# One encoder step on one core: the values of 32 sample tokens for three mLSTM heads, computed as an fp32 product on four column parts of TensorE

## The chip, the cores and the metric

The kernel runs on one NeuronCore of one Trainium2 chip. The metric is the time on the device of one execution, in microseconds; smaller is better. It is given as the median of several runs. Beside the runs, one execution was recorded by the hardware profiler, and all rows of a trace below are from such an execution.

## The reference

The reference is one inference step of a two-layer streaming encoder. Two groups of tokens go through the same weights: a prompt of 1024 tokens and a sample of 32 tokens, 1056 together, with 1024 features each. Layer 0 is an mLSTM mixer with four heads and an MLP, layer 1 is chunk-band attention and an MLP. The change lies in the mixer's values `v`:

```
def mlstm_mixer(u, conv_prev, C0, n0, m0, w_in, b_if, conv_w, conv_b, mhn_g, w_out, chunk_len):
    proj = u @ w_in
    qk_pre = proj[..., :2 * QK_A]
    v = proj[..., 2 * QK_A:2 * QK_A + V_A]
    o_pre = proj[..., 2 * QK_A + V_A:2 * QK_A + 2 * V_A]
...
    vh = v.astype(jnp.float32).reshape(Bsz, S, NH_A, DV_A)
...
    h, C, n, m = mlstm_scan(q, k, vh, ig, lf, C0, n0, m0, chunk_len)
```

`u` is the modulated input (1056 tokens by 1024), `w_in` the input weight (1024 by 3080), and each head's values are 256 columns of it. All of it is float32.

## The kernel before

All large products are made from split operands. A float32 array is split into a high part and a rest, both in the type fp32r (`split`, L85 to L90: the high part is a cast on ScalarE, the rest a subtraction on VectorE), and a product is the sum of three matmuls: high by high, high by rest, rest by high. The tile `U` holds both parts of `u` with the features on the partitions: 8 chunks of 128 features, 1056 tokens each, and 96 zero columns behind them.

A weight is fetched by `wtile` (L92 to L104): a DMA on SyncE's queue brings 512 rows into a tile of the ring `raw` (three buffers), and the split writes both parts into a tile of the ring `wc` (six buffers). While the mixer runs, one of the three raw buffers is held by the accumulator of a modulation vector (`ada_acc`), so two are left for weights; the tile `cl`, through which a head's old state comes in, is taken from the same ring.

The mixer runs head by head. For heads 2 to 4 (the loop's h = 1 to 3; a head's number here is h + 1) three things are in flight at once. `qk_proj(h)` makes the head's queries and keys. `v_proj(h)` (L498 to L506) then makes its values: nine blocks of tokens, eight of 128 and a last one that holds the 32 sample tokens, and for each block 24 matmuls by `v_chunk` (L483 to L489), 8 feature chunks by 3 split terms, with 128 tokens of `U` as the stationary operand and 256 weight columns as the moving one. The last block also loads 128 columns of `U`: the 32 sample tokens and 96 columns behind them, whose rows of the result nobody reads. `v_out` (L491) copies a finished block on ScalarE from PSUM to a tile `vt`. Meanwhile the generator `mlstm(h-1)` (L639 on) does the scan of the head before, one chunk of 128 tokens at a time: scores `S` (L668, L669), numerator `num` (L686, L688), state update `cu` (L690), the normalisation on VectorE and ScalarE (`sm`, `hn`, L715 to L731), and the transposes `hT` on TensorE (L738). A `Flow` object gives the generators a tick after each block; `v_proj` calls `after(t)` behind each of its nine blocks.

The values of head 1 are made earlier by `v_first`, interleaved with the input's transposes, with the same `v_chunk`. After head 4's values comes `o_proj`, the output gate.

The order in which the program is written is not the order in which it runs. A scheduler in the build orders each engine's instructions by its own cost model, within the dependencies, so an instruction that depends on nothing late can move far. On each engine, instructions then run strictly in that order: an instruction that waits for a semaphore holds up everything behind it, on TensorE, VectorE, ScalarE, GpSimd and on SyncE's queue of DMAs alike. PSUM tiles come from small rings too: three buffers `mm` for projection blocks, two `nm` for `num` and `cu`, two `tp` for scores and transposes.

At the kernel's start `ada_mm` (L432 to L436) forms a modulation vector as fp32 products with a stationary of 32 columns, `cs`, placed on four column parts of the array by the partitions they write (0, 32, 64 and 96).

Of the kernel before, what the change touches and what calls it, by code (L numbers as in the profile page):

```python
# [8 lines left out]
F32 = mybir.dt.float32  # L9
F32R = mybir.dt.float32r  # L10
# [5 lines left out]
P = 128  # L16
D = 1024
KC = D // P
TP = 1024
TS = 32  # L20
T = TP + TS
NT = T // P + 1
# [53 lines left out]
def trunk_kernel(ctx: ExitStack, tc: tile.TileContext, a, o):  # L76
    nc = tc.nc
    flow = Flow()
    cp = ctx.enter_context(tc.tile_pool(name="const", bufs=1, reuse_waits="tile"))
# [12 lines left out]
    def wtile(name, srcs, ncols=256, pool=None, eng=None, between=None):  # L92

        raw = raw_tile([P, 4, ncols], f"raw_{name}")
        for dst, src in srcs(raw):
            nc.sync.dma_start(dst, src)
        if pool is None:
            w = ring.tile([P, 2, 4, ncols], F32R, tag="wc", name=f"w_{name}", bufs=6)
        else:
            w = pool.tile([P, 2, 4, ncols], F32R, tag="h", name=f"w_{name}", bufs=5)  # L100
        if between:
            between()
        split(w[:, 0], w[:, 1], raw, eng)
        return w  # L104

# [23 lines left out]
    nc.vector.tensor_add(sel, ident[:, 0:32], ident[:, 32:64])  # L129
    for i in (64, 96):  # L130
        nc.vector.tensor_add(sel, sel, ident[:, i:i + 32])
    ones_d = cp.tile([P, P], F32R, name="ones_d")
    nc.vector.memset(ones_d.bitcast(F32), 1.0 / D)
    eps_ln = cp.tile([P, 1], F32, name="eps_ln")
    nc.vector.memset(eps_ln, LN_EPS)
    eps_hn = cp.tile([P, 1], F32, name="eps_hn")
# [10 lines left out]
    NPT1, NPT2 = 112, 112  # L147
    pt1 = cp.tile([P, NPT1], F32, name="pt1")
    pt2 = cp.tile([P, NPT2], F32, name="pt2")
    cs = cp.tile([P, KC, 32], F32, name="cs")  # L150
    ada = cp.tile([P, NPT2, 2], F32, name="ada")
    bif = cp.tile([36, 1], F32, name="bif")
    nc.vector.memset(bif, 0.0)
# [19 lines left out]
    def mmt(name):  # L173
        return pa.tile([P, 512], F32, tag="mm", name=name, bufs=3)
# [32 lines left out]
    adaw = [ada_load(k) for k in range(4)]  # L207
# [158 lines left out]
    up_cm = tc.tile_pool(name="upool", bufs=1, side="right", reuse_waits="tile")  # L366
    upool = up_cm.__enter__()
    UF = KC * T
    U = upool.tile([P, 2 * UF + 96], F32R, name="U")
    nc.vector.memset(U[:, 2 * UF:].bitcast(F32), 0.0)  # L370

    def uap(hl, k, t0, n):
        off = hl * UF + k * T + t0
        return U[:, off:off + n]

# [56 lines left out]
    def ada_mm(k):  # L432

        for q in range(4):
            nc.tensor.matmul(ada_ps[32 * q:32 * q + 32, :512], cs[:, k, :], adaw[k][:, q * 512:(q + 1) * 512],
                             start=(k == 0), stop=(k == KC - 1))  # L436

    def ada_first():
# [31 lines left out]
    G = None  # L470
    cst = {}

    def v_weight(h, half):
# [7 lines left out]
        return wtile(f"v{h}_{half}", srcs, 264 if h == 0 else 256)  # L481

    def v_chunk(ps, ws, t, k):  # L483
        w = ws[k // 4]
        n = w.shape[-1]
        uh, ul = uap(0, k, t * P, P), uap(1, k, t * P, P)
        nc.tensor.matmul(ps[:, :n], uh, w[:, 0, k % 4, :], start=(k == 0), stop=False)
        nc.tensor.matmul(ps[:, :n], uh, w[:, 1, k % 4, :], start=False, stop=False)
        nc.tensor.matmul(ps[:, :n], ul, w[:, 0, k % 4, :], start=False, stop=(k == KC - 1))  # L489

    def v_out(ps, h, t):  # L491
        m = P if t < NT - 1 else TS
        vt = A.tile([P, 258], F32, tag="vt", name=f"vt_{h}_{t}", bufs=9)
        nc.scalar.copy(vt[:m, :256], ps[:m, :256])
        nc.gpsimd.memset(vt[:m, 256:258], 1.0)
        if h == 0:
            nc.vector.tensor_copy(bass.AP(g64.tensor, g64[:m, t, 0:4].offset, [g64[:m].ap[0], [32, 2], [1, 4]]),
                                  ps[:m, 256:264].rearrange("p (a b) -> p a b", a=2))  # L498
        return vt

    def v_proj(h, after):
        ws = [v_weight(h, half) for half in range(2)]
        vts = []
        for t in range(NT):
            ps = mmt(f"v_{h}_{t}")
            for k in range(KC):  # L506
                v_chunk(ps, ws, t, k)
            vts.append(v_out(ps, h, t))
            after(t)
        return vts  # L510

    def v_first(ws, nxt):

# [278 lines left out]
    def next_u(bi, k):  # L792
# [7 lines left out]
                        pass  # L800
        flow.tick()
    vts = [v_first(vw, next_u)]
    for t0, n in TBS:
        nc.sync.dma_start(xsp[0][:, :, t0:t0 + n], xt[:, :, t0:t0 + n])
    flow.finish()
# [68 lines left out]

    T_cm = tc.tile_pool(name="temps", bufs=1, reuse_waits="tile")
    T_ = T_cm.__enter__()

    def tmp_t(shape, name, dt=F32):
        return T_.tile(shape, dt, tag="t", name=name, bufs=5)
# [1287 lines left out]
```

## Time and profile before

| quantity | value |
|---|---|
| median of three runs | 2407.8 us (2407.55, 2407.8, 2413.93) |
| the profiled execution's own time | 2412.41 us |
| its span | 2410.6 us |
| mean granted TensorE clock | 0.995 |
| PE busy | 2342.7 us, 97% of the span |
| DVE busy | 1939.0 us, 80% |
| ACT busy | 1206.0 us, 50% |

PE is TensorE's matmul side and PEld its weight loads, DVE is VectorE, ACT is ScalarE, POOL is GpSimd and SP is SyncE with its DMA queue. The span is the time from the first to the last recorded instruction; the 1.8 us by which the profiled execution's own time is longer lies around it. In a row of the timeline the first number is the start in us from the span's start, the second the duration in us, then engine, line, operation, output and inputs, shape and count (x2 where two equal ones in a row are put together), and in brackets how long the engine sat idle before it and what ended that.

### The profile page before, as it was taken

The numbers are of one execution on the slowest core, as the hardware profiler recorded it, in microseconds if no ns is written. First come the engines' busy times: TensorE is split into PE (matmuls) and PEld (weight loads), VectorE is DVE, ScalarE is ACT, GpSimd is POOL, SyncE is SP. The second block draws the span as 40 slices with busy tenths as digits, with TensorE's granted clock in tenths as the row PEclk, the third lists the DMA queues.
The fourth block names the chain that finished last, engine by engine and source line by source line (L and its number), as shares of the span: only waits on it lengthen the run. The fifth ranks groups of instructions, "written<-read, shape, count | busy, mean of one in ns | idle before, by whom it ended". The sixth has DMA issues, their size and how long they took to land. (4 is left out here: it accounts for less than half of the span.)

```text
span 2410.6 us, 44188 instructions
## 1 busy us (share of the span) xinstructions
PE 2342.7 (97%) x17180; PEld 2250.4 (93%) x17180; DVE 1939.0 (80%) x3903; ACT 1206.0 (50%) x2454; POOL 168.1 (7%) x320
## 2 busy tenths in 40 slices
PE   7999999999999999999999999999999999899997
PEld 4999999999999999999999987789999999899997
DVE  4888766778788789989888777756998889888778
ACT  4565557278666630101147467773776777222212
POOL 0111100000000000000000224420000000000003
PEclk9999999999999999999999999999999999999999
DMA  8343222526566896675512330051486779976642
GB/s 302 120 131 103 78 89 66 177 91 206 184 198 200 279 336 230 252 261 215 183 56 89 82 93 1 10 140 59 165 278 211 259 278 335 355 256 236 224 146 73
DMA packets 284277, 424.64 MB, mean 176 GB/s; under 512 B 15384, under 2 KB 205228, under 8 KB 278948
## 3 DMA queue, kind: packets, MB, share of 16 engines
q1 hardware_dynamic: 279860, 391.48, 48.3%
q10 hardware_dynamic: 4208, 30.35, 3.1%
q8 instruction: 135, 2.21, 0.4%
q14 instruction: 74, 0.61, 0.1%
HBM read 305.96 MB, written 118.17 MB: 176 GB/s over the span
## 5 line engine op out<-in xcount | busy, mean ns | idle before, releaser
L1082 DVE SCALAR_TENSOR_TENSOR ACX<-dn,ada,ACX 128x264 f32<-128x264 f32 (+6 forms) x664 | 281.8, 447 | 83.2 <-PE dn L1452 41.1
L1452 PE MATMUL dn<-fx,wf_d 128*128 128x264 f32 x2016 | 254.1, 285 | 6.8 <-DVE ACX L1082 3.5
L1452 PEld LDWEIGHTS dn<-fx,wf_d 128*128 128x128 f32 x2016 | 248.8, 188 | 9.0 <-DVE ACX L1082 3.0
L89 ACT CAST w_dn<-raw_dn 128x1024 fp32r<-128x1024 f32 x36 | 37.7, 1050 | 282.1 <-DVE aw L279 136.9
L118 PE MATMUL dn<-hs,w_dn 128*128 128x384 f32 (+2 forms) x512 | 161.2, 315 | 0.0
L119 PE MATMUL dn<-hs,w_dn 128*128 128x384 f32 (+2 forms) x512 | 161.0, 315 | 0.0
L120 PE MATMUL dn<-hs,w_dn 128*128 128x384 f32 (+2 forms) x512 | 156.4, 314 | 1.3 <-DVE w_dn L90 1.3
L1317 PE MATMUL up<-TF,wf_u 128*128 128x264 f32 x1056 | 143.2, 285 | 3.8 <-ACT H L1320 3.8
L1317 PE MATMUL up<-U,wf_u 128*128 128x264 f32 x1056 | 140.3, 285 | 1.7 <-ACT H L1320 1.2
L1317 PE MATMUL up<-u,wf_u 128*128 128x264 f32 x1056 | 139.7, 285 | 1.3 <-ACT wf_u L89 0.7
L279 DVE SCALAR_TENSOR_TENSOR aw<-radw,cs,aw 128x512 f32<-128x512 f32 x196 | 139.5, 743 | 1.1 <-DMA radw<-in_w_ada_dram 1.1
L1317 PEld LDWEIGHTS up<-TF,wf_u 128*128 128x128 f32 x1056 | 134.4, 189 | 4.8 <-ACT H L1320 4.6
L1317 PEld LDWEIGHTS up<-U,wf_u 128*128 128x128 f32 x1056 | 133.0, 188 | 3.0 <-ACT H L1320 1.6
L1317 PEld LDWEIGHTS up<-u,wf_u 128*128 128x128 f32 x1056 | 132.9, 188 | 1.9 <-ACT wf_u L89 0.9
L118 PE MATMUL dn<-U,w_dn 128*128 128x384 f32 (+2 forms) x416 | 129.4, 312 | 0.6 <-DVE ada L304 0.6
L119 PE MATMUL dn<-U,w_dn 128*128 128x384 f32 (+2 forms) x416 | 129.4, 312 | 0.0
L120 PE MATMUL dn<-U,w_dn 128*128 128x384 f32 (+2 forms) x416 | 125.9, 313 | 0.6 <-DVE w_dn L90 0.5
L1817 ACT ACTIVATE p<-p,mx 128x576 f32<-128x576 f32 (+9 forms) x132 | 86.6, 657 | 27.5 <-DVE mx L1814 25.2
L120 PEld LDWEIGHTS dn<-hs,w_dn 128*128 128x128 f32 x512 | 96.0, 188 | 2.0 <-DVE w_dn L90 1.8
L118 PEld LDWEIGHTS dn<-hs,w_dn 128*128 128x128 f32 x512 | 96.5, 189 | 0.1
L119 PEld LDWEIGHTS dn<-hs,w_dn 128*128 128x128 f32 x512 | 96.6, 189 | 0.0
L90 DVE TENSOR_TENSOR HL<-H,HL 128x1056 fp32r<-128x1056 f32 x64 | 80.3, 1254 | 20.0 <-ACT HL L89 19.9
(403 smaller groups left out, 7111.0 us busy)
## 6 DMA issues: line engine op xcount, KB each, us to landing
hpl<-HL SPq DMA_DIRECT2D x144, 264.0 KB
rdn_u<-in_w_up_dram SPq DMA_DIRECT2D x64, 512.0 KB
hd<-HL SPq DMA_DIRECT2D x28, 1056.0 KB
fx<-hd SPq DMA_DIRECT2D x50, 528.0 KB
radw<-in_w_ada_dram SPq DMA_DIRECT2D x24, 1024.0 KB
hd<-HM SPq DMA_DIRECT2D x28, 792.0 KB
raw_up<-in_w_up_dram SPq DMA_DIRECT2D x40, 512.0 KB
raw_dn<-in_w_down_dram SPq DMA_DIRECT2D x36, 512.0 KB
```

Of the source, the lines that this page charges most:

```text
L89: nc.scalar.copy(dst_h, src)
L90: (eng or nc.vector).tensor_sub(dst_l, src, dst_h.bitcast(F32))
L118: nc.tensor.matmul(ps, wh, mov(0, k), start=(k == 0), stop=False)
L119: nc.tensor.matmul(ps, wh, mov(1, k), start=False, stop=False)
L120: nc.tensor.matmul(ps, wl, mov(0, k), start=False, stop=(k == nk - 1))
L279: nc.vector.scalar_tensor_tensor(acc[cnd], raw[:, k], sc, acc[cnd], op0=ALU.mult, op1=ALU.add)
L1082: nc.vector.scalar_tensor_tensor(xs, ps[:, off + o:off + o + mm_], gate[:, fc, cnd:cnd + 1], xs, op0=ALU.mult, op1=ALU.add)
L1317: nc.tensor.matmul(p, self.ws[w][:, wl, k], moving(f, tp, xl, k), start=first and k + n_ == 0, stop=k == 3 and n_ == 2, skip_group_check=n ...
L1452: nc.tensor.matmul(p, ws[w][:, wl, k], t[:, s0, xl], start=first and k + n_ == 0, stop=k == kg - 1 and n_ == 2, skip_group_check=not first)
L1817: nc.scalar.activation(z, z, AF.Exp, bias=mx[:, 0:1], scale=-1.0, accum_out=mx[:, 1:2])
```

## The change

The sample's block of values for heads 2 to 4 is no longer the ninth block of split matmuls. It is the first thing that `v_proj` does. `v_sample` runs, for each half of the weight, four fp32 products with the raw, unsplit weight as the moving operand (256 columns) and 32 columns `us` as the stationary one, one product for each of four feature chunks, each on a column part of its own, so that two halves are eight products and the four parts of one PSUM tile hold partial sums over two chunks each. `wtile` now passes the raw tile to `between`, and so these products are issued behind the weight's DMA and ahead of its split. `v_out` adds the parts up: the copy on ScalarE takes part 0, and three additions on VectorE of 32 by 256 from PSUM take the others. `us`, the sum of both parts of `u` for the sample tokens, is made once by one VectorE addition into the wider constant tile `cs`.

With it come smaller edits. The blocks of values live in a ring of eight `vt` and a ring of two `vs`, where there was one of nine. `v_first` still makes the sample's block with 24 split matmuls, but its stationary has 32 columns, not 128; so the 96 zero columns of `U` and their memset go. `ones_d`, a constant that the layer norms use later, is made in a later pool, by a memset after the mixer. `v_proj` gives the same nine ticks; the ninth now comes right behind the eighth.

```
-            between()
+            between(raw)
...
-    cs = cp.tile([P, KC, 32], F32, name="cs")
+    cs = cp.tile([P, KC, 2 + TS], F32, name="cs")
+    us = cs[:, :, 2:]
...
-    U = upool.tile([P, 2 * UF + 96], F32R, name="U")
-    nc.vector.memset(U[:, 2 * UF:].bitcast(F32), 0.0)
+    U = upool.tile([P, 2 * UF], F32R, name="U")
...
     def v_chunk(ps, ws, t, k):
-        uh, ul = uap(0, k, t * P, P), uap(1, k, t * P, P)
+        m = P if t < NT - 1 else TS
+        uh, ul = uap(0, k, t * P, m), uap(1, k, t * P, m)
+        ps = ps[:m]
...
+    def v_sample(us, ps, half, raw):
+        for k in range(4):
+            nc.tensor.matmul(ps[32 * k:32 * k + 32, :256], us[:, 4 * half + k], raw[:, k], start=(half == 0),
+                             stop=(half == 1))
...
     def v_out(ps, h, t):
-        vt = A.tile([P, 258], F32, tag="vt", name=f"vt_{h}_{t}", bufs=9)
+        vt = A.tile([P, 258], F32, tag="vt", name=f"vt_{h}_{t}", bufs=8) if m == P else \
+            A.tile([P, 258], F32, tag="vs", name=f"vt_{h}_{t}", bufs=2)
         nc.scalar.copy(vt[:m, :256], ps[:m, :256])
+        if m < P and h:
+            for q in range(1, 4):
+                nc.vector.tensor_add(vt[:m, :256], ps[32 * q:32 * q + m, :256], vt[:m, :256])
...
     def v_proj(h, after):
-        ws = [v_weight(h, half) for half in range(2)]
+        ps = mmt(f"v_{h}_s")
+        ws = [v_weight(h, half, lambda raw: v_sample(us, ps, half, raw)) for half in range(2)]
+        vs = v_out(ps, h, NT - 1)
         vts = []
-        for t in range(NT):
+        for t in range(NT - 1):
...
-        return vts
+        after(NT - 1)
+        return vts + [vs]
...
     vts = [v_first(vw, next_u)]
+    uv = U.rearrange("p (i k t) -> p i k t", i=2, t=T)[:, :, :, TP:].bitcast(F32)
+    nc.vector.tensor_add(us, uv[:, 0], uv[:, 1])
```

The scheduler's order differs between the two programs from head 1's values up to `o_proj`; behind that each engine has the same instructions in the same order, but for the memset of `ones_d`. Three places in head 3's value phase show what moved. The names end in a running number of the tile; `w_v_0` and `raw_v_0` are the first half of the value weight, `v_0` is the first block of 128 tokens, and `hT_0`, `num_4`, `S_5` belong to chunks 0, 4 and 5 of head 2's scan.

TensorE, where head 3's value phase begins, before:

```order
L686 MATMUL num_4_2321<-vt_4_1705,sT_4_2220 128x257
L688 MATMUL num_4_2321<-ct_3_2231,qc_4_2222 128x257
L690 MATMUL cu_4_2324<-vt_4_1705,kw_4_2224 128x257
L487 MATMUL v_0_2348<-w_v_0_2340,U 128x256
L488 MATMUL v_0_2348<-w_v_0_2340,U 128x256
L489 MATMUL v_0_2348<-w_v_0_2340,U 128x256
```

and after, the same place; the later lines are from the second half of the same first block:

```order
L703 MATMUL cu_4_2309<-vt_4_1718,kw_4_2209 128x257
L494 MATMUL v_s<-raw_v_0_2324,cs 32x256 x4
L494 MATMUL v_s<-raw_v_1_2333,cs 32x256 x4
L487 MATMUL v_0_2348<-w_v_0_2326,U 128x256
...
L489 MATMUL v_0_2348<-w_v_1_2335,U 128x256
L751 MATMUL hT_0_2225<-ident,hn_0_2015 128x128 x2
L487 MATMUL v_0_2348<-w_v_1_2335,U 128x256
L488 MATMUL v_0_2348<-w_v_1_2335,U 128x256
L751 MATMUL hT_1_2229<-ident,hn_1_2094 128x128 x2
```

The eight products of the sample's block stand ahead of the first block, both raw halves are read there, and the transposes `hT_0` and `hT_1`, which stood in the second block before, now stand in the first.

SyncE's queue, the next weights (`raw_qk`, head 4's queries and keys) and the old state `cl` of head 2, before:

```order
L750 DMA out_dram<-co_7_1809 128x2x128 [waits Activation_49]
L657 DMA cl_2510<-in_state_C_dram 128x2x128 [waits DMAHW3_49,DVE_49]
L750 DMA out_dram<-co_8_1844 128x2x128 [waits Activation_49]
L263 DMA ada_room<-in_w_ada_dram 128x4x512 [waits DMAHW0_49,DVE_49]
L96 DMA raw_qk_0_2778<-in_w_in_a_dram 128x4x128 [waits DMAHW4_49,DMAHW1_49,DVE_49]
```

and after:

```order
L262 DMA ada_room<-in_w_ada_dram 128x4x512 [waits DMAHW0_49,DVE_49]
L763 DMA out_dram<-co_8_1857 128x2x128 [waits Activation_49]
L262 DMA ada_room<-in_w_ada_dram 128x4x512 [waits DMAHW6_49,DVE_49]
L670 DMA cl_2510<-in_state_C_dram 128x2x128 [waits DMAHW3_49,DMAHW1_49,PE_49]
L96 DMA raw_qk_0_2750<-in_w_in_a_dram 128x4x128 [waits DMAHW4_49,DMAHW2_49,PE_49]
```

Both DMAs reuse raw buffers that held the value weight; before they waited for its split on VectorE, now for TensorE's sample products, which read it last.

VectorE, between `sT_5` and the statistics of chunk 5 (`st_5`), before; the split that stands there is of a half of head 4's `w_v`:

```order
L290 TENSOR_REDUCE cx<-ada_room 128x2x8 x2
L671 TENSOR_TENSOR sT_5_2315<-S_5_2312,W_5_2310 128x128
L90 TENSOR_TENSOR w_v_0_3192<-raw_v_0_3190,w_v_0_3192 128x1024
L462 SCALAR_TENSOR_TENSOR sl_0_2282<-y_2277,sl_0_2282 128x353
L462 SCALAR_TENSOR_TENSOR sl_353_2289<-y_2277,sl_353_2289 128x353
L705 BN_STATS st_5_2394<-num_5_2387 128x6
```

and after:

```order
L684 TENSOR_TENSOR sT_5_2300<-S_5_2297,W_5_2295 128x128
L719 BN_AGGR sm_3_2218<-st_4_2313 128x2
L504 TENSOR_TENSOR vt_8_2342<-v_s,vt_8_2342 32x256
L90 TENSOR_TENSOR w_qk_0_2753<-raw_qk_0_2750,w_qk_0_2753 128x1024
L504 TENSOR_TENSOR vt_8_2342<-v_s,vt_8_2342 32x256
L718 BN_STATS st_5_2394<-num_5_2387 128x6
L460 SCALAR_TENSOR_TENSOR sl_0_2267<-y_2262,sl_0_2267 128x353
```

The three additions of the sample's parts lie around the split of `w_qk_0`, and that split, which stood further ahead before, is now the one that stands between `sT_5` and `st_5`. `vt_8` is the sample's tile.

More of the change, by code (lines that the diff above doesn't have):

```diff
@@ L131, in trunk_kernel @@
         nc.vector.tensor_add(sel, sel, ident[:, i:i + 32])
-    ones_d = cp.tile([P, P], F32R, name="ones_d")
-    nc.vector.memset(ones_d.bitcast(F32), 1.0 / D)
     eps_ln = cp.tile([P, 1], F32, name="eps_ln")
@@ L434, in ada_mm @@
         for q in range(4):
-            nc.tensor.matmul(ada_ps[32 * q:32 * q + 32, :512], cs[:, k, :], adaw[k][:, q * 512:(q + 1) * 512],
+            nc.tensor.matmul(ada_ps[32 * q:32 * q + 32, :512], cs[:, k, 0:32], adaw[k][:, q * 512:(q + 1) * 512],
                              start=(k == 0), stop=(k == KC - 1))
@@ L471, in trunk_kernel, with v_weight @@
     cst = {}
-    def v_weight(h, half):
+    def v_weight(h, half, between=None):
         def srcs(raw):
@@ L480, in srcs @@
             return r
-        return wtile(f"v{h}_{half}", srcs, 264 if h == 0 else 256)
+        return wtile(f"v{h}_{half}", srcs, 264 if h == 0 else 256, between=between)
     def v_chunk(ps, ws, t, k):
@@ L876, in trunk_kernel @@
     T_ = T_cm.__enter__()
+    ones_d = T_.tile([P, P], F32R, name="ones_d")
+    nc.vector.memset(ones_d.bitcast(F32), 1.0 / D)
     def tmp_t(shape, name, dt=F32):
```

## The prediction, on record before the changed kernel ran

> **What bounds the kernel now.** I read the page's totals first, then the table of windows over the mixer, then the list of what TensorE waited for in it, then single rows of the timeline. The totals:
>
> ```profile
> span 2410.6 us, 44188 instructions
> PE 2342.7 (97%) x17180; PEld 2250.4 (93%) x17180; DVE 1939.0 (80%) x3903; ACT 1206.0 (50%) x2454; POOL 168.1 (7%) x320
> ```
>
> TensorE is busy for 97% of the span. The change lies in the mixer, so what counts is whether that holds there. The windows give length, then busy time of PE, PEld, DVE, ACT and POOL, then the granted clock; the value phases of heads 2, 3 and 4 begin at 127, 201 and 270 us:
>
> ```profile
> 120.00:160.00 40.00, 38.70 (x273) 35.65 (x271) 38.74 (x96) 28.33 (x85) 9.73 (x25) 1.00 0.37 114
> 200.00:240.00 40.00, 38.57 (x286) 35.10 (x285) 33.03 (x85) 22.87 (x65) 6.16 (x23) 1.00 0.42 134
> 280.00:320.00 40.00, 39.64 (x282) 36.59 (x281) 17.37 (x59) 21.92 (x64) 3.06 (x13) 1.00 0.32 104
> 310.00:340.00 30.00, 29.95 (x171) 28.97 (x169) 22.61 (x57) 15.72 (x41) 2.27 (x3) 1.00 0.31 104
> ```
>
> PE fills 38.6 to 39.6 of 40 us in all three, so it bounds each. But VectorE is as full as PE in head 2's phase (38.74), has 7 us of room in head 3's and 22 in head 4's. The list of waits says how little PE stood still between 66 and 340 us (total, times, longest), and its three rows say where:
>
> ```profile
> PE hT L738 <- ACT hn L731: 2.8, 3, 1.3
> 155.87 0.44 PE L738 MATMUL hT<-ident,hn 128*128 128x128 f32 x2 [1.19 <-ACT hn L731]
> 222.27 0.33 PE L738 MATMUL hT<-ident,hn 128*128 128x128 f32 x1 [1.25 <-ACT hn L731]
> 296.20 0.33 PE L738 MATMUL hT<-ident,hn 128*128 128x128 f32 x1 [0.36 <-ACT hn L731]
> ```
>
> One such wait falls in each value phase, 1.19, 1.25 and 0.36 us. Time taken off PE is therefore worth nearly its full length here, as long as the scan's chain on VectorE and ScalarE, which ends these waits, does not take it back.
>
> **The change part by part.** *What TensorE loses.* The price of a block is read at the end of head 4's phase, where nothing lies between the last three blocks: the first matmul of block 7, the last of the sample's block, and the two instructions after it.
>
> ```profile
> 298.78 0.39 PE L487 MATMUL v<-w_v,U 128*128 128x256 f32 x1
> 307.18 0.28 PE L489 MATMUL v<-w_v,U 128*128 128x256 f32 x1
> 307.39 0.26 PE L301 MATMUL adas<-cx,sel 128*32 128x16 f32 x8
> 307.59 0.44 PE L118 MATMUL o<-U,w_o 128*128 128x384 f32 x1
> ```
>
> From 298.78 to 307.18 the 71 steps between 72 matmuls take 8.40 us, 0.118 each, so a block of 24 is 2.84 us. Three sample blocks go: 3 x 2.84 = 8.5 us.
>
> *What TensorE gains in work.* The nearest row for four column parts is the modulation vector at the start, eight records for four parts in two passes of 512 columns:
>
> ```profile
> 24.83 1.06 PE L435 MATMUL ada<-rada,cs 128*32 128x512 f32 x8
> ```
>
> The four parts with both passes end within 1.06 us, so the parts run side by side. A head's sample block is two such groups of 256 columns instead of one of 512: the same columns per part, so 1.06 us, and 3 x 1.06 = 3.2 us in all. The lower end comes from whole-array fp32 products of 257 columns that follow each other, and so does the upper:
>
> ```profile
> 119.68 0.60 PE L686 MATMUL num<-vt,sT 128*128 128x257 f32 x2
> 120.12 0.60 PE L690 MATMUL cu<-vt,kw 128*128 128x257 f32 x2
> ```
>
> One product takes 0.44 us (120.12 less 119.68). If the parts are fully in step, a head pays 2 x 0.44 = 0.88; if they do not overlap at all, 8 x 0.44 = 3.5 us, more than the block that goes. The row of L435 is of the very shape, so I take 1.06.
>
> *Switching.* The row of L301 is a group on four column parts in the midst of a full stream, with only 16 columns to move. It begins 0.21 us after the matmul ahead of it (0.118 is the step within a block), and the next instruction 0.20 later: 0.09 + 0.20 = 0.3 us for going to column parts and back, little of it the group's own work. A head goes there once, since its eight products stand together: 3 x 0.3 = 0.9 us. The bounds are 0.1 a head (the first step alone) and 0.3 for each half, 1.8. The Trainium skill, "TensorEngine Tiling (Array Packing)", section Key Properties, says that a change of the tiling mode drains the array, which speaks against short groups such as these; it has no price, and the 0.3 us here agree with it.
>
> PE's own sum is -8.5 + 3.2 + 0.9 = -4.4 us, with ends -8.5 + 2.6 + 0.3 = -5.6 and, serially, -8.5 + 10.6 + 0.9 = +3.0.
>
> *VectorE's additions.* Three of 32 by 256 per head from PSUM; the nearest rows are a 128-column product and a 257-column update that read PSUM:
>
> ```profile
> L671 DVE TENSOR_TENSOR sT<-S,W 128x128 f32<-128x128 f32 x24 | 6.8, 284 | 5.1 <-PE S L669 5.1
> L693 DVE SCALAR_TENSOR_TENSOR ct<-ct,albc,cu 128x257 f32<-128x257 f32 x24 | 11.4, 473 | 1.9 <-PE cu L690 1.8
> ```
>
> Between 3 x 0.28 = 0.85 and 3 x 0.47 = 1.4 us a head; I take 1.2, nearer the row with as many columns. In heads 3 and 4 VectorE's room hides them. In head 2 there is 1.3 us of room in 40, so this cover can fail: up to 1.2 us. The chunk whose `vt` they make comes last in the scan, so nobody waits for the result itself; but they hold a PSUM buffer `mm` until the third is through, and the third block of values needs it.
>
> *The weight that is fetched later.* The sample's products read the raw tiles, so `cl` and `raw_qk_0` now wait for PE, and on SyncE's queue `raw_qk_1`, the rows `rc` and the modulation's weights stand behind them. What a fetch takes, and what follows:
>
> ```profile
> 200.26 0.37 SPq L96 DMA_DIRECT2D raw_v<-in_w_in_a_dram  x1
> 203.84 1.05 ACT L89 CAST w_v<-raw_v 128x1024 fp32r<-128x1024 f32 x1 [3.87 <-DMA raw_v<-in_w_in_a_dram]
> 207.40 0.28 DVE L671 TENSOR_TENSOR sT<-S,W 128x128 f32<-128x128 f32 x1
> 207.60 1.21 DVE L90 TENSOR_TENSOR w_v<-raw_v,w_v 128x1024 fp32r<-128x1024 f32 x1
> 212.16 0.28 DVE L671 TENSOR_TENSOR sT<-S,W 128x128 f32<-128x128 f32 x1
> ```
>
> A fetch is 3.6 us from issue to cast, a cast 1.05, and from a split's start to the end of the next `sT` there are 4.84 us (207.60 to 212.44). In head 3, counted from the phase's start: products done at 1.1, fetch issued by about 1.5, cast from 5.1, split from 6.2, two additions more behind it (0.6 to 0.9), so the next `sT` is ready between 11.6 and 12. On PE, 58 value matmuls (7.0), the sample's 1.1, and 15 pieces of the scan at 0.22 to 0.44 (about 4) stand ahead of the numerator that needs it: 12. That is even, with up to 1 us of new wait, and the same again at the third block's PSUM buffer, out of the same chain. In head 2 the queue's `raw_qk` had long come:
>
> ```profile
> 111.58 0.94 SPq L96 DMA_DIRECT2D raw_qk<-in_w_in_a_dram  x2
> ```
>
> It was issued 16 us ahead of the phase, and now can't be before about 1.5 us into it; its user is the next phase, some 40 us later, so only the cast's place in ScalarE's order can hurt. In head 4 the same holds for the output gate's weights.
>
> *The old waits.* With blocks and transposes reordered, the 2.8 us of `hT` waits may go, stay or move. They are ended by a chain of VectorE and ScalarE rows that the change makes longer, not shorter. I set old waits that go against new ones that come, net zero, from -2.8 to +3.
>
> *At no cost:* the one addition that makes `us` (0.3 to 0.5 us of VectorE, hidden by PE work until the first value phase some 30 us later or more); the memset of `ones_d`, in a stretch where VectorE has 7.4 of 30 us free; the ninth tick, which moves no PE work; the smaller `U`. The 32-column stationary in head 1's sample block changes nothing if moving columns set the pace, and they do:
>
> ```profile
> 100.16 0.34 PE L118 MATMUL qk<-U,w_qk 128*128 128x384 f32 x1
> 100.34 0.34 PE L119 MATMUL qk<-U,w_qk 128*128 128x384 f32 x1
> ```
>
> 0.18 us for 384 columns and 0.12 for 256 are the same per column. Uncovered, all of these are below 1 us.
>
> The sum is -4.4 us. The profiled execution took 2412.41 us (its span and 1.8 around it), so 2408.0 in its own terms; the median of the runs is 4.6 below that execution, so I put the same difference on the median: 2407.8 - 4.4 = **2403.4 us**.
>
> **The rivals.** *The waits go too.* If the new order also removes the `hT` waits, the gain is 5.6 + 2.8 = 8.4 at most and 4.4 + 2.8 = 7.2 by the sum; between them, 7.8, the time is 2400.0. For it speaks that `hT_0` now has cover in another place; against, that VectorE's rows ahead of it grew.
>
> *The scan's chain takes it back.* If a chain on VectorE and ScalarE, not PE, sets the length of a value phase, the chain keeps its length and gets 1.2 us of additions per head: the gain of 1.5 a head is lost in heads 2 and 3, and head 2 pays 1.2 on top: 2407.8 - 1.5 + 1.2 = 2407.5. Head 2's 38.74 of 40 speaks for it there; VectorE's room in heads 3 and 4 against it.
>
> *The parts don't run side by side* next to a full stream, so that the change doesn't do what it says: +3.0, 2410.8. The L435 row speaks against.
>
> *Slower: PE stands still long enough to lose its clock.* The place is the raw ring: the late `raw_qk` holds ScalarE at the cast, the scan's rows behind it are late, and PE waits for `sT` or `hT`. What a long wait costs stands ahead of head 2's keys:
>
> ```profile
> 92.02 1.13 PE L577 MATMUL ae_ps<-ident,stk 36*128 36x36 f32 x9 [2.42 <-ACT stk L570]
> 93.56 0.52 PE L120 MATMUL qk<-U,w_qk 128*128 128x384 f32 x1
> 93.88 0.52 PE L118 MATMUL qk<-U,w_qk 128*128 128x384 f32 x1
> 97.95 0.44 PE L118 MATMUL qk<-U,w_qk 128*128 128x288 f32 x1
> ```
>
> After 2.42 us of idling a 384-column matmul takes 0.32 us instead of 0.18, until about 98: 5 us at that pace lose 5 x (1 - 0.18/0.32) = 2.2 us, with the wait 4.6. It decides from a wait of about 2.4 us in each of the three heads: 3 x 4.6 - 4.4 = +9.4, 2417. The shorter waits at 155.87 and 222.27 were not followed by slow matmuls, as a row behind the first of them shows:
>
> ```profile
> 156.26 0.28 PE L489 MATMUL v<-w_v,U 128*128 128x256 f32 x1
> ```
>
> It lasts 0.28 us, as the one at 307.18 does in a full stream, and my count finds 1 us of waiting, not 2.4. The Trainium skill, "TensorE: Matmul & The Clock Gate", Part 1, puts the clock's fall behind an idle window of about 3.4 us; by that a wait would have to be longer still, and the trace shows the slow rows after 2.42 us and a group of small transposes.
>
> **How the numbers follow.** My forecast (PE's sum, waits net zero within 2.5 us) gets 0.55, the waits gone 0.17, the chain taking it back 0.16, parts in series 0.05, the lost clock 0.07. The forecast's own spread is 2400.9 to 2405.9; the range reaches down into the first rival and up through the second towards the third: 2398 to 2410. About 0.3%, 7.2 us, is what a measurement of this kernel can tell from no change; faster than that means below 2400.6, slower above 2415. Most of the first rival and a small part of the forecast lie below: faster 0.2. The lost clock, and a corner of the series case: slower 0.07. Within: 0.73.
>
> **What would show it.** In the profile after: value phases without the ninth block, so 24 matmuls of L487 to L489 fewer each; two groups of four products at the start of each phase, together 0.9 to 1.1 us from the first to the next block's first matmul, about 1.4 with the switches; additions of 0.28 to 0.47 us; PE's waits between 66 and 340 us in sum near 2.8 and none over 2 us; the clock at 1.00 in all value phases; and `o_proj` beginning about 4.4 us earlier, with everything behind it shifted as a whole. I am wrong if the products take 3 us a head, if the list of waits shows `sT`, `vt` or a cast ahead of PE with 2 us or more, or if the gain at `o_proj` is given back behind it.

## The result, and the profile after

The changed kernel is slower: 2413.93 us in the median of 22 runs (2411.32 to 2419.49), against 2407.99 (2405.52 to 2415.74) in 22 runs of the kernel before beside it. The ratio is 1.0021, with a 95% interval of 1.0015 to 1.0027: 5 us lost by the ratio (5.9 between the medians) where 4.4 were to be gained, and outside the range of 2398 to 2410. It is less than the 7.2 us that the prediction took as the least difference that can be told from no change; the 22 runs on each side resolve less than that.

The first profile of the change is no slower than that of before: both have a span of 2410.6 us, but the execution of the change lies 1.5 us under the median of its runs, that of before 4.4 above. So the profiles are read for what happens in the mixer, and three more of the change and two more of before were taken. The page's totals for the first of the change:

```profile
span 2410.6 us, 44151 instructions
PE 2336.1 (97%) x17156; PEld 2241.0 (93%) x17156; DVE 1939.8 (80%) x3912; ACT 1206.8 (50%) x2454; POOL 168.9 (7%) x320
```

PE is busy for 6.6 us less. The same windows as before show where that went:

```profile
120.00:160.00 40.00, 36.64 (x265) 33.23 (x263) 35.98 (x91) 24.48 (x75) 7.75 (x19) 1.00 0.40 124
200.00:240.00 40.00, 36.44 (x283) 32.34 (x283) 28.91 (x79) 24.34 (x68) 5.25 (x23) 1.00 0.46 143
280.00:320.00 40.00, 38.62 (x278) 35.82 (x277) 25.55 (x67) 22.55 (x59) 3.07 (x13) 1.00 0.41 130
```

PE now stands still for 3.4 of 40 us in head 2's phase (1.3 before), 3.6 in head 3's (1.4 before) and 1.4 in head 4's (0.4 before). The list of its waits from 66 to 340 us, which had one kind of row in these phases, 2.8 us in all, has three of weight:

```profile
PE hT L751 <- ACT hn L744: 7.0, 7, 1.8
PE cu L703 <- ACT sm L722: 1.6, 1, 1.6
PE v L487 <- DVE vt L504: 1.4, 1, 1.4
```

The work on TensorE is, in sum, what was forecast. In head 3's phase the eight products (sixteen records of two passes) stand in one piece, from their first row to the next block's first:

```profile
202.28 1.07 PE L494 MATMUL v_s<-raw_v,cs 128*32 128x256 f32 x16
203.28 0.39 PE L487 MATMUL v<-w_v,U 128*128 128x256 f32 x1
```

That is 1.00 us with the way in and out. In heads 2 and 4 the group is cut in two by a piece of the scan, and its parts take 0.55 + 1.00 and 0.98 + 0.57 us. Together 4.1 us, as forecast (3.2 + 0.9), but partly by luck: a group in one piece takes 0.4 us less than the 1.06 + 0.3 that were put for it, and two of the three groups are not in one piece.

A table over all profiles sets gain against loss. "Values to op_a" is the time on PE from the start of head 2's values to the first product behind the output gate (op_a), and the next column what PE waited in it (waits over 0.1 us). Between the brackets of a ratio is its 95% interval; each kernel was timed beside the kernel before on the same chip. In early, head 2's products stand ahead of head 2's values and so outside of this stretch.

| kernel | median, us (before beside it) | ratio | values to op_a, us | waits in it, us |
|---|---|---|---|---|
| before (3 profiles) | | | 293.1, 294.3, 293.3 | 3.9, 5.1, 4.1 |
| the change (4 profiles) | 2413.93 (2407.99) | 1.0021 (1.0015 to 1.0027) | 295.6, 293.1, 298.5, 294.2 | 11.4, 8.1, 10.0, 9.9 |
| rest_only | 2410.01 (2408.76) | 1.0003 (0.9994 to 1.0012) | 293.7 | 4.8 |
| sample_only | 2413.64 (2408.76) | 1.0017 (1.0009 to 1.0026) | 293.6 | 9.3 |
| no_sample | 2405.21 (2408.76) | 0.9988 (0.9980 to 0.9997) | 286.1 | 5.6 |
| parts_from_split | 2406.61 (2408.76) | 0.9990 (0.9981 to 0.9999) | 289.6 | 3.1 |
| rest_hold | 2415.04 (2408.67) | 1.0025 (1.0016 to 1.0034) | 294.6 | 5.9 |
| no_adds | 2408.00 (2408.67) | 1.0003 (0.9994 to 1.0012) | 290.2 | 6.2 |
| split_first | 2406.54 (2408.67) | 0.9993 (0.9984 to 1.0002) | 290.5 | 3.7 |
| tick_first | 2412.14 (2408.67) | 1.0007 (0.9998 to 1.0016) | 292.1 | 6.7 |
| early (2 profiles) | 2415.28 (2407.43) | 1.0032 (1.0022 to 1.0042) | 293.5, 291.3 | 8.4, 9.0 |
| split_noadds | 2409.07 (2407.43) | 1.0004 (0.9995 to 1.0013) | 292.0 | 5.3 |

In the mean over profiles this stretch takes 295.3 us in the change and 293.6 before. Its waits grew from 4.4 to 9.8 us (+5.4). Stretch less waits, PE's work, is 289.1 us in each profile of before and 284.2 to 285.0 in three of the change: 4.6 us less, beside 4.4 forecast. The fourth has 288.6, and that execution shows the granted clock falling in head 4's phase (windows of 10 us, the granted clock third from the right; a wait of 1.75 us for hT ends at 291.20):

```profile
280.00:290.00 10.00, 9.45 (x70) 8.92 (x68) 9.49 (x28) 4.18 (x12) 2.27 (x7) 1.00 0.49 164
290.00:300.00 10.00, 8.80 (x38) 5.85 (x38) 4.72 (x14) 5.90 (x16) 0.93 (x6) 0.63 0.35 105
300.00:310.00 10.00, 10.00 (x74) 9.82 (x73) 2.13 (x7) 4.73 (x14) 0.00 (x0) 0.85 0.14 41
```

### The profile page after: what moved, and what is told of

Read it like the earlier page. It is cut to its first block, busy times and chain, and to the rows that moved or that the text cites. A ratio compares the mean times of both kernels' runs of the same rounds, so it can differ in the third digit from the quotient of the medians.

```text
span 2410.6 us, 44151 instructions
## 1 busy us (share of the span) xinstructions
PE 2336.1 (97%) x17156; PEld 2241.0 (93%) x17156; DVE 1939.8 (80%) x3912; ACT 1206.8 (50%) x2454; POOL 168.9 (7%) x320
```

## The experiments

Three theories went in. A: the sample's products and additions bring the waits that eat the gain, by the raw tiles that they hold or by VectorE's added rows. B: the other edits cost, behind the mixer. C: the scan's chain on VectorE and ScalarE sets the length of a value phase, so that PE's saved work is worth little.

**Which part of the change (rest_only, sample_only).** rest_only puts the sample's block back in the ninth place with 24 split matmuls; sample_only is the kernel before with the sample's block alone:

```
# rest_only, in v_proj
-        ws = [v_weight(h, half, lambda raw: v_sample(us, ps, half, raw)) for half in range(2)]
-        vs = v_out(ps, h, NT - 1)
-        for t in range(NT - 1):
+        ws = [v_weight(h, half) for half in range(2)]
+        for t in range(NT):
```

> The changed kernel with the sample's block made as before, by 24 split matmuls in the ninth place; all other edits stay. Theory A (the sample's products and additions bring the waits that eat the gain, all inside the mixer): 2408, within 1.5 us of the kernel before, and PE's waits between 66 and 310 us again about 5 us. Theory B (the other edits, through moved tiles or order, cost about 4 us behind the mixer): 2412 to 2413. Theory C (PE has less work, but the scan's chain on VectorE and ScalarE sets the length of a value phase): 2408, as A.

> The kernel before with the sample's block alone as in the change; the rings of vt, the 96 zero columns, head 1's stationary and the constant of the layer norms stay as before. Only the ninth block's vt ring is the old one of nine. Theory A: 2412 to 2414 as the whole change, waits between 66 and 310 us about 12 us. Theory B: the mixer alone, whose end is 1.4 us later in the profile, so 2408 to 2409.5. Theory C: as A.

rest_only is level with before and sample_only slower by 4.1 us (0.17% of 2408.76). The list of waits of sample_only, from 118 to 420 us, has the kinds of the change:

```profile
PE hT L751 <- ACT hn L744: 6.8, 6, 1.6
PE cu L703 <- ACT sm L722: 1.4, 1, 1.4
PE v L488 <- DVE vt L504: 0.8, 1, 0.8
```

Theory B falls as the account of the change: the sample's block carries the loss.

**No sample block at all (no_sample).** Products, copy and additions are left out and a memset fills the tile:

```
-        ps = mmt(f"v_{h}_s")
-        ws = [v_weight(h, half, lambda raw: v_sample(us, ps, half, raw)) for half in range(2)]
-        vs = v_out(ps, h, NT - 1)
+        ws = [v_weight(h, half) for half in range(2)]
+        vs = A.tile([P, 258], F32, tag="vs", name=f"vt_{h}_{NT - 1}", bufs=2)
+        nc.gpsimd.memset(vs[:TS], 1.0)
```

> The changed kernel without any work on the sample's block for heads 2 to 4: no products, no copy, no additions; a memset takes their place, so the sample's outputs are left out. The ninth tick stays behind the eighth block. Theory A: the waits go back to about 5 us and PE's 8.5 us come off in full, 2399 to 2401. Theory C: the scan's chain keeps its length, PE waits 8 us more than before, and the time is 2406 to 2410. Theory B: 4 us above what A gives, 2403 to 2405.

Values to op_a shrink by 7.5 us, with 1.2 us more waiting, so in the mixer the freed work does come through, and C holds for a small part only. But the timed gain is only 2.9 us (0.7 to 4.8): 2405.21 us lies between what A and C forecast, and nearest to B's 2403 to 2405. So 4 to 5 us are missing from the time in a kernel that neither reads a raw tile on TensorE nor adds parts. A lower clock may account for a part of them: the mean granted clock of its 11 runs is 0.9943, that of the 33 runs of the kernel before beside it 0.9956, and 0.0013 of 2405 us are, by estimate, 3 us of full speed. Why its clock is lower is not shown.

**Raw tiles not held (parts_from_split, split_first).** Both make the block with sixteen fp32 products on four column parts that read the split weights, 1.87 us a head. parts_from_split has them in the ninth place, split_first ahead of the first block:

```
+        for g in range(2):
+            for wl in range(2):
+                for q in range(4):
+                    nc.tensor.matmul(ps[32 * q:32 * q + 32, :256], us[:, 4 * g + q], ws[g][:, wl, q].bitcast(F32),
+                                     start=(g == 0 and wl == 0), stop=(g == 1 and wl == 1))
```

> The changed kernel with the sample's block in the ninth place again, on four column parts, but as sixteen fp32 products that read the split weights (high part and rest one after the other), so that the raw tiles come free at the split as before; additions and copy stay. PE work is about 1 us a head more than in the change (2 us instead of 1). Theory A with the raw ring as the main cause: 2408 - 8.5 + 6 + 1 = 2406, waits of about 5 to 7 us, and none of a cast or cu behind a late fetch. If the additions are the main cause: 2411 or more, waits as in the change. Theory C: 2409 to 2411, with the waits of hT as in the change. Theory B: 2410.

> The kernel parts_from_split with its sixteen products put first in the value phase, as the change has them, and the ninth tick behind the eighth block; the raw tiles still come free at the split. With the raw ring as the main cause: within 1.5 us of parts_from_split, 2405 to 2408. If the place of the block (first, and no PE work under the last tick) is the cause: 2410 to 2413, with waits of hT at the start of the next phase as in the change.

Although they work longer on PE than the change does, both are about 7 us faster than it (0.9990 and 0.9993 against 1.0021), parts_from_split faster than before as well. The waits of split_first from 118 to 420 us:

```profile
PE hT L753 <- ACT hn L746: 2.8, 5, 1.1
PE hT L753 <- DVE ct L677: 0.5, 1, 0.5
```

The waits of cu and v are gone. The place of the block makes no difference that shows; whether TensorE reads the raw tiles does. These kernels can't tell whether that is because the tiles are held longer.

**The hold alone (rest_hold).** rest_only with one product of four columns per half, whose result nobody reads:

```
+        hold = mmt(f"v_{h}_s")
+        ws = [v_weight(h, half, lambda raw: nc.tensor.matmul(hold[:32, :4], us[:, 0], raw[:, 0, :4], start=True,
+                                                             stop=True)) for half in range(2)]
```

> The kernel rest_only, whose sample block is the old one in the ninth place, with one thing added: for each half of the value weight one tiny fp32 product of 4 columns reads the raw tile, in the place where the change puts its sample products; its result is used by nobody. So the raw tile is held as in the change, with next to no work on PE and none on VectorE. Theory A with the raw ring as the main cause: 3 to 4 us above rest_only, 2413, and the wait of cu behind a late fetch in head 2's phase is there (about 1.5 us). If the additions or the early place are the cause: 2409 to 2411, as rest_only.

It costs 5 us against rest_only (1.0025 against 1.0003; the intervals don't meet), with next to no work on any engine. What it moves is seen in SyncE's queue. In rest_only the old state and the next weights of head 3's phase are fetched here:

```profile
163.19 0.37 SPq L664 DMA_DIRECT2D cl<-in_state_C_dram  x1
170.06 0.92 SPq L96 DMA_DIRECT2D raw_qk<-in_w_in_a_dram  x2
```

in rest_hold here, behind the phase's start, as in the change (202.98 and 203.45):

```profile
202.60 0.37 SPq L666 DMA_DIRECT2D cl<-in_state_C_dram  x1
203.07 1.06 SPq L96 DMA_DIRECT2D raw_qk<-in_w_in_a_dram  x2
```

In head 2's phase raw_qk goes from 110.72 to 128.08. So the ring loses a whole query phase of prefetch, 17 to 33 us. In head 2's phase the late fetch holds ScalarE at the cast, the copy to `sm` behind it is late, and cu waits for the PSUM buffer that this copy frees:

```profile
132.20 1.05 ACT L89 CAST w_qk<-raw_qk 128x1024 fp32r<-128x1024 f32 x1 [2.54 <-DMA raw_qk<-in_w_in_a_dram]
133.91 0.70 PE L699 MATMUL cu<-vt,kw 128*128 128x257 f32 x2 [0.70 <-ACT sm L718]
```

Leaving aside the two runs with splits on GpSimd, the profiles agree on this link: in each kernel whose value phase reads the raw tiles on TensorE (the change in all four profiles, sample_only, rest_hold, no_adds, tick_first) this cast stands at 132 to 136 us and waits 0.9 to 2.8 us for the fetch, and cu waits 0.7 to 1.6 us. In the three profiles of before, in rest_only, no_sample, parts_from_split, split_first and split_noadds the cast of the same half runs at 114 to 115 us, waits 0.35 us at most, and no cu waits in that phase.

But cu's wait in rest_hold, 0.70 us where about 1.5 was expected, is a small part of its 5 us. Its profile is 3.5 us longer than that of rest_only. From the start of head 1's values to that of head 2's it takes 1.4 us more, where the clock took longer to come back after the wait of ae_ps; this is not the hold's doing, since the kernel before shows both lengths too (92.0 us in one profile, 90.7 in two). Up to op_a it is 0.9 us more (1.1 more of waits), and 1.7 behind op_a, within the spread given below. So the 5 us are measured, but most of them are not located.

**The additions (no_adds, split_noadds).** Both lose the loop of three additions, so that a quarter of the sum is kept:

```
-        if m < P and h:
-            for q in range(1, 4):
-                nc.vector.tensor_add(vt[:m, :256], ps[32 * q:32 * q + m, :256], vt[:m, :256])
```

> The changed kernel without the three additions: only the first of the four partial sums is kept, so the sample's values of heads 2 to 4 lack three quarters of their sum. If the additions are the main cause: 2409 or less, the wait of a value block for vt (1.4 us) gone and the others halved. With the raw ring as the main cause: 2412 to 2413, that wait gone, the wait of cu in head 2's phase still there.

> The kernel split_first without the three additions: the sample's values of heads 2 to 4 lack three quarters of their sum. In the changed kernel the additions were worth about 4 us (no_adds against the whole). If they cost that by themselves: 2402 to 2403. If they cost it only together with a raw tile that is held, because they then stand in a queue behind a late split: within 1.5 us of split_first, 2405 to 2407.

In the change they are worth 4 us (1.0003 against 1.0021). The 2408.00 us are what was expected of the additions as the main cause, not of the raw ring, though the waits are those expected for the raw ring: that for vt is gone, that of cu in head 2's phase is still there (1.5 us). So neither carries the loss alone. As a sum, 4.6 us less of PE's work, 5 for the hold (rest_hold) and 4 for the additions make a loss of 4.4, beside 5 measured.

In split_first, without the hold, taking the additions out gains nothing (1.0004 against 0.9993); split_noadds, at 2409.07, lies above both of its forecasts, and why is open. So the additions show no price where the tiles are not held. In the same way no_adds and split_noadds, with and without the hold, are level, though split_noadds has 2.7 us more work on PE: by this pair the hold is worth about 3 us, give or take as much. That the additions cost because they stand with late splits in one queue is read from the traces and not shown by a run of its own.

**The ninth tick (tick_first).**

```
         vs = v_out(ps, h, NT - 1)
+        after(NT - 1)
...
-        after(NT - 1)
         return vts + [vs]
```

> The changed kernel with the ninth tick of a value phase moved from behind the eighth block to right behind the sample's products. If the last tick without PE work under it is what leaves transposes of hT to the next phase (waits at 173 and 236 us): these waits go, 2411 or less. With the raw ring as the main cause: 2413 to 2415, the same or worse, since the scan is asked for earlier.

1.0007, with the wait at the start of the next phase (1.4 us at 173 in the change) gone and hT down to 3.1 us, but four waits of cu (2.8 us) and one of num (0.7) in its place. The wait at 236 (1.1 us) lies inside head 3's value phase, almost 5 us ahead of its end, and the same transposes still wait 0.98 us, at 230.98. So the tick's place explains one of the two, not the sum; against 1.0021 it looks like a gain of 3 us, but the two intervals still touch.

**Released in time by an early issue (early).** The same products, copy and additions, at the start of the query phase:

```
     def qk_proj(h, after, pre=None):
         ws = [wtile(f"qk{h}_{i}", srcs(512 * i)) for i in range(2)]
+        if pre:
+            pre.append(v_early(h))
```

> The changed kernel with the same eight products, copy and additions, issued one phase earlier: at the start of the head's query and key phase instead of its value phase, about 31 to 57 us sooner. The raw tiles of the value weight, which are there by then, come free that much earlier, long before cl and the next raw_qk need them. Theory A with the raw ring as the main cause: PE's gain of 8.5 - 4.1 comes through, 2403 to 2406, below the kernel before by more than its interval, and no cu waits behind a late cast in head 2's value phase. If the additions cost 4 us by themselves, wherever they stand: 2408 to 2410. If the price lies in having PE read the raw tiles at all: 2412 to 2414.

> The kernel early once more, for a profile: if its 7.7 us come from the wait of hT near 160 us (2.7 us) and the fall of the clock behind it, both are here again, and the stretch from head 2's queries to o_proj is 238 us; without the fall it is 233 to 234.

This went against the theory: 1.0032, the slowest of the series that keeps the work on its engines, and nearest to what was expected if the price lies in having PE read the raw tiles at all (2412 to 2414). The fetches of cl and the next raw_qk in head 3's phase do come back ahead of it (173.58 and 174.10). But now head 3's value weight is late in head 2's phase, and its split stands between two rows of the scan's normalisation on VectorE:

```profile
154.66 0.16 DVE L742 TENSOR_TENSOR sm<-sm 128x3 f32<-128x3 f32 x1
154.84 1.05 ACT L89 CAST w_v<-raw_v 128x1024 fp32r<-128x1024 f32 x1 [2.98 <-DMA raw_v<-in_w_in_a_dram]
155.92 1.23 DVE L90 TENSOR_TENSOR w_v<-raw_v,w_v 128x1024 fp32r<-128x1024 f32 x1 [1.10 <-ACT w_v L89]
157.06 1.05 DVE L743 TENSOR_TENSOR sm<-sm 128x3 f32<-128x3 f32 x1
...
159.97 0.44 PE L755 MATMUL hT<-ident,hn 128*128 128x128 f32 x2 [2.71 <-ACT hn L748]
```

ScalarE waits 2.98 us for the fetch, VectorE 1.10 for the cast, the row sm that stands behind it starts 2.2 us after the one ahead has ended, and PE waits 2.71 for hT. Then the clock falls:

```profile
140.00:160.00 20.00, 17.29 (x132) 16.48 (x130) 17.51 (x46) 9.85 (x29) 4.65 (x11) 1.00 0.48 161
160.00:180.00 20.00, 20.00 (x111) 15.96 (x112) 13.22 (x35) 9.72 (x28) 0.91 (x4) 0.74 0.43 125
```

Both are back in the second profile (a wait of 3.01 us, a clock of 0.91; 236.6 us from head 2's queries to o_proj, where 238 was expected). So holding the tiles is one way to a late fetch, not the only one. That reading the raw tiles on PE costs something by itself is not ruled out: no run reads them there without moving a fetch. Of early's 7.7 us, about 2 are there at op_a (422.6 and 421.1 us from the span's start, against 419.7 in the mean of before). The mean granted clock of its runs is 0.9950 against 0.9960 of before beside it, by the estimate used above 2.4 us, to which falls like this one belong; the rest is not located.

**The splits off VectorE (after_pool, rest_pool).** The rest part of the next weights' split on GpSimd (`eng=nc.gpsimd`), in the change and in rest_only:

> The changed kernel with the rest part of the split of the value weights of heads 2 to 4 and of the query and key weights of heads 3 and 4 made on GpSimd and no longer on VectorE. If the late splits in VectorE's queue, ahead of the scan's rows, are what eats the gain: below the changed kernel by 3 us or more and below rest_pool, since PE's 4.4 us come through, with hT waits of 1.3 us or less. If PE's gain is lost whatever VectorE does: at or above rest_pool. GpSimd may be slow enough to become a wait of its own (a value block waiting for w_v); then both this kernel and rest_pool are slower than without it, and the test says nothing.

> The same move to GpSimd in rest_only, which has the sample's block in the old form, as the control for after_pool: 2406 to 2412.

Inconclusive: 2427.49 and 2428.16 us, ratios 1.0075 and 1.0078. A split takes GpSimd 2.5 us, and the control loses as much as the test.

**Profiles again (before_2, before_3, after_2, after_3, after_4).**

> The kernel before, unchanged, for a second profile. Its first profiled execution took 2412.4 us, 4 us above the median of its runs, and the changed kernel's 2412.45, 1.5 below its own. If what the first profile lost lies behind the mixer, as the comparison of all profiles suggests, head 2's queries begin at 70.4 us and o_proj at 307.6 (within 0.5) here as well, and the time from there to the end is 2099 to 2103 us.

> The kernel before once more, for the spread between profiles of one kernel: o_proj at 307.6 (within 0.5), from there to the end 2099 to 2103 us.

> The changed kernel, unchanged, for a second profile. If the mixer's course is fixed by order and waits: o_proj begins at 308.5 (within 0.5), with the waits of cu, v and hT where the first profile has them. If the change also slows what lies behind the mixer: from there to the end 2103 to 2106 us, longer than in the kernel before; if not, the same as there.

> The changed kernel once more, for the spread between profiles of one kernel: o_proj at 308.5 (within 0.5), from there to the end 2103 to 2106 us if the change slows later stages, else as before_2 and before_3.

> The changed kernel once more, for a profile: from the start of head 2's queries at 70.2 us to o_proj 235.7 to 240.8 us, as in the three before; the upper end if the granted clock falls once between 110 and 310 us.

The mixer's course is not fixed: o_proj begins at 307.6, 306.7 and 306.1 us before and at 308.5, 305.9, 311.0 and 307.5 in the change, 311.0 being the one with the fallen clock. So the expectation that it begins within 0.5 us of the first profile failed for both kernels. The same kinds of waits are there in each, at 0.2 to 1.8 us. From o_proj to the end the three profiles of before take 2100.7 to 2103.0 us, as expected, and the four of the change 2102.1 to 2105.9, two of them as expected if the change slows what lies behind the mixer. From op_a to the end it is 1990.3, 1987.4, 1988.9 before and 1989.2, 1991.5, 1991.2, 1989.5 in the change: 1.5 us more in the mean, with 1987 to 1993 over all kernels.

## Why the prediction was wrong, point by point

*PE's own sum* was right in its total: 8.5 us go, 4.1 come (with two errors that cancel, as said above), and PE's work up to op_a is 4.6 us less. The column parts ran side by side; the rival in which they don't is out.

*The additions* take 0.42 us each, nine in all (forecast 0.4). That they would hold a PSUM buffer which the third block needs, with up to 1 us, was right in mechanism: in the four profiles that block waits 0.3 to 1.4 us. In the first, the third addition is over at 212.47, behind the split of w_qk, and the block of values waits for it.

```profile
208.74 1.49 DVE L90 TENSOR_TENSOR w_qk<-raw_qk,w_qk 128x1024 fp32r<-128x1024 f32 x1 [0.94 <-ACT w_qk L89]
210.26 0.42 DVE L504 TENSOR_TENSOR vt<-v_s,vt 32x256 f32<-32x256 f32 x1
212.04 0.43 DVE L504 TENSOR_TENSOR vt<-v_s,vt 32x256 f32<-32x256 f32 x1
212.52 0.39 PE L487 MATMUL v<-w_v,U 128*128 128x256 f32 x1 [1.44 <-DVE vt L504]
```

*The weight that is fetched later* was named, and its place in head 2 undersized: "its user is the next phase, some 40 us later, so only the cast's place in ScalarE's order can hurt". It hurt. The cast, which ran at 115.2 us before, stands early in ScalarE's order of the value phase and waits for the fetch; everything behind it is late, at last the copy that frees cu's buffer:

```profile
129.09 2.16 SPq L96 DMA_DIRECT2D raw_qk<-in_w_in_a_dram  x2
134.09 1.05 ACT L89 CAST w_qk<-raw_qk 128x1024 fp32r<-128x1024 f32 x1 [1.73 <-DMA raw_qk<-in_w_in_a_dram]
138.62 1.20 DVE L90 TENSOR_TENSOR w_qk<-raw_qk,w_qk 128x1024 fp32r<-128x1024 f32 x1
140.31 0.48 PE L703 MATMUL cu<-vt,kw 128*128 128x257 f32 x1 [1.59 <-ACT sm L722]
```

*The failed step* is "I set old waits that go against new ones that come, net zero, from -2.8 to +3". The old ones stayed at the same transposes (only the smallest, 0.36 us, shrank), and with the new ones the waits grew by 5.4 us in the mean, beyond the +3 that bounded the term. In each head the forecast priced one late fetch by itself; what the traces show is that cast, split, additions and the scan's rows share two strict queues, so that one late fetch moves a row that PE needs in several places. By timed runs, reading the raw tiles on TensorE in the value phase costs 5 us (rest_hold), and the additions 4 more beside it (no_adds); with either left out the loss is gone (split_first, no_adds). How the time is lost is shown for the fetch, the cast and cu, by all profiles; that the late split is the link between fetch and scan is read from the traces, and shown in early by its rows; the runs with the split on GpSimd, which were to show it by itself, said nothing. Each of these kernels is also ordered anew by the scheduler, so two of them differ in more than the edit; what that alone is worth is not shown. And the step accounts for the lost gain, not for the whole loss: the waits' 5.4 us against 4.6 of work, and the fallen clock of one profile, make the stretch up to op_a 1.7 us longer in the mean, of 5 us timed.

*The rivals.* The chain that takes the gain back, at 0.16, is the nearest by its time (2407.5). But that the chain keeps its length does not hold, since in no_sample the freed work came through in the mixer; and its price was too small: 1.5 us each in heads 2 and 3 and 1.2 more in head 2, where the waits grew by 5.4. The lost clock, at 0.07, had the path that the traces show: the late raw_qk holds ScalarE at the cast, and the scan's rows behind it are late. Its price was wrong: it was put behind a wait of 2.4 us in all three heads. It fell in one of four profiles of the change, after 1.75 us, and cost 4 us there (288.6 against 284.5), and in both of early.

*Behind the mixer.* The forecast was that o_proj begins 4.4 us earlier and everything behind it shifts as a whole. It begins 1.4 us later in the mean (308.2 against 306.8). Of the 4 us between the means of the profiled executions (2414.5 and 2410.4), 2.5 are there at op_a and 1.5 behind it, no more than the spread. In rest_hold, no_sample and early the timed runs give 4 to 6 us more loss (or less gain) than the profiles show up to op_a. Some of that gap comes from the executions that were profiled: those of before took 1.1 to 4.4 us more than the median of its runs. For the change, the mean granted clock of the 22 runs is 0.9952, where the runs of before beside the other kernels have 0.9954 to 0.9960: by estimate 0.5 to 2 us. SyncE's order with its waits is the same there in before and after. What is left stays open.

## What to carry to other kernels

Before an operation is put on an operand that is only a way station (a raw tile ahead of a split), ask what its ring does next: a reader in a later phase holds the buffer until then, and the fetches that are queued for it wait as well, here by 17 to 33 us. Price a late fetch not by its user alone but by everything that stands behind its cast and split in the strict queues of their engines. And even next to an engine that is full at 97% with short waits, ask what the change adds to the chain beside it: here 5.4 us of new waits ate the 4.6 us of saved work.

## What the runs showed of the hardware

The granted clock fell after a wait shorter than the 2.42 us seen before: in the third profile of the change after 1.75 us (at 291.20), with transposes and products of 32 rows among the work behind it, for some 10 us. Longer waits left it at 1.00: 1.80 us in the first profile of the change (160.32), 1.92 in the second of before (155.08) and 1.94 in rest_hold (222.88). So did 1.53 us at the same place in the fourth profile of the change (291.77). The Trainium skill, "TensorE: Matmul & The Clock Gate", Part 1, ties the fall to an idle window of about 3.4 us; these rows don't agree with a wait of that length as the condition, and what else entered was not tried.

A group of sixteen fp32 records on four column parts, 256 columns each, took 1.00 us in a full stream with the way in and out (head 3). Beside the 0.88 of two products in step that leaves, by estimate, about 0.1 us for both changes of the tiling. Cut in two by other work, the same group took 1.55 us (heads 2 and 4).
